# Four packed block products build the delta rule's 128x128 inverse, which is then applied in one product

## The chip, the core and the metric

The kernel runs on one core of a Trainium2 chip. The core has a matrix engine (TensorE, PE in the profile; its weight loads are listed as PEld), a vector engine (DVE), a scalar engine (ACT), a general one (POOL), and a queue that issues DMAs (SP). Each engine works through its own queue in order, and waits for the others by semaphores. A matrix product reads a stationary operand (the weights, 128 rows by up to 128 columns) and a moving operand from SBUF and writes to PSUM; the other engines bring the result from there to SBUF.

The metric is the device time of one execution in microseconds. Lower is better.

## What is computed

One layer of a hybrid encoder over 256 tokens of width 2048: RMSNorm; a wide input projection that feeds retention (8 heads) and a gated delta rule (16 heads of width 128); gates and an output projection; cross-attention to 256 memory tokens; a squared-ReLU MLP of hidden width 8192; a last RMSNorm. All in float32. The change is inside the delta rule, which the reference states by chunks:

```python
kb = kc * bc
m = jnp.where(strict, jnp.einsum("nbhid,nbhjd->nbhij", kb, kc) * decay, 0.0)
t = lax.linalg.triangular_solve(eye + m, jnp.broadcast_to(eye, m.shape),
                                left_side=True, lower=True, unit_diagonal=True)
u = t @ (vc * bc)
w = t @ (kb * jnp.exp(cum_g)[..., None])
qk = jnp.einsum("nbhid,nbhjd->nbhij", qc, kc) * decay
...
v_new = u_i - w_i @ state
o = (q_i * jnp.exp(g_i)[..., None]) @ state + qk_i @ v_new
```

Put for a whole sequence, each head has to solve a unit lower triangular system (I + M) y = r, where M holds the decayed products of keys, and then to form o from y. The kernel does this with tiles of 128 tokens (two tiles, `NT` = 2).

## The kernel before

**The stream.** Most of the work is products of activations with weights read from HBM. `fetch` (L89 on) loads a piece of weights (`raw`), rounds it on ACT to a high part (`whi`, L108) and takes the rest on DVE (`wlo`, L111), with three buffers of each; `chunk` and `blocks` then issue the products on PE (L151 to L153, and L193 and L194). `blocks` of two output blocks is a run of pairs, one product of 512 columns (L193) and one of 256 (L194).

**The order.** A scheduler with its own model of the engines puts every engine's instructions in order. `fetch` has a high priority there. Work that is not stream is mixed into it: a generator in the list `steps` is advanced by `step()`, twice in each group of weights, up to its next `yield`; `finish_steps()` runs what is left.

**The delta rule.** The loop near the end of the mixer runs over four groups `j` of four heads:

- `gdn_stream(j)` projects q, k, v of the group, forms the products of keys and of queries with keys, and writes them, scaled and decayed, to one tile `alt` for each head (four buffers). `diag(alt)` is the part that lies within a 128-token tile, with M transposed in it. The four 32x32 blocks on the diagonal are copied to `cmp_l`, and the right sides r to `r4`.
- `gdn_blocks(j)` sends `cmp_l` through DRAM so that each of the 32 blocks (4 heads, 2 tiles, 4 blocks) has a partition of its own, inverts them there by 31 steps of forward substitution on DVE (L650, L652), sends them back through DRAM to `ct` (one DMA for each of four groups of 32 partitions, L657), and transposes each block to `cu` (L659). Then DVE spreads them over block-diagonal 128x128 tiles `t0` and `u0` (L667, with the mask `bd32`) and clears the diagonal blocks of `diag(alt)` (L671, with the mask `offd`).
- `gdn_core(j)` is the generator that goes into `steps`. With T the block-diagonal inverse and N = M_off T, where M_off is M without its diagonal blocks, the inverse is T (I - N)(I + N N), since N to the fourth is zero. For each tile it forms N once (L681, copied to `am` on ACT, L682), and then applies N three times and T once to the 128x128 right side of each head: w = N r (copied on ACT, L702), sq = r + N w (DVE, L704), sq = sq - N sq (DVE, L706), y = T sq (ACT, L708). The second tile first has the first one's part taken off (L699). Last, the outputs are formed from y, normalised and scaled for both tiles (L718 to L728).

Each such application goes through `times` (L689): four products, one for each head, of 128 columns, float32. One float32 product stands in the trace as two weight loads and two matrix instructions, so one call of `times` is eight of each. A core has twelve stretches between its `yield`s.

The first core (j = 0) is put into `steps` after its gates, so it runs beside `gdn_stream(1)`; the others run beside their own retention gates. `finish_steps()` in the next `gdn_stream` and before the last gates closes what is still open.

**Other lines that come up.** L374 and L375 build `bd32` on POOL, L377 to L379 build `offd` on DVE; L228 is the first matrix instruction; L593 is a product with a single column (a sum of squares of q); `PAD1` (L36) is an empty tile that moves the addresses behind it in the pool `kv`, which is closed before the mixer's pool `mix` is opened.

Of the kernel before, what the change touches and what calls it, by code (L numbers as in the profile page):

```python
# [10 lines left out]
F32 = mybir.dt.float32  # L11
F32R = mybir.dt.float32r
I32 = mybir.dt.int32
AF = mybir.ActivationFunctionType
ALU = mybir.AluOpType
AX = mybir.AxisListType

P = 128
D = 2048
S = 256  # L20
NT = S // P
# [3 lines left out]
GH, GD = 16, 128  # L25
# [9 lines left out]
PAD1, PAD2 = 8, 80  # L35
# [16 lines left out]
def trunk(ctx: ExitStack, tc: tile.TileContext, x, mem, positions, norm_mix_g, w_in, conv_w, gdn_a_log, gdn_dt_bias,  # L52
          ret_gn_g, gdn_norm_g, w_out, norm_x_g, norm_mem_g, w_xq, w_xkv, w_xo, norm_ffn_g, w_ff1, w_ff2,
          norm_final_g, inv_freq, out):
    nc = tc.nc
    PSUM = bass.MemoryType.PSUM
    act, vec, pool, pe = nc.scalar, nc.vector, nc.gpsimd, nc.tensor
# [14 lines left out]
    def bank():  # L72
        return psp.tile([P, 512], F32, name="b", tag="b", bufs=4)
# [135 lines left out]
    ones = cp.tile([P, P], F32, name="ones")  # L209
# [163 lines left out]
    bd32 = mc.tile([P, 4], F32, name="bd32")  # L373
    pool.affine_select(bd32, ones[:, :4], pattern=[[-32, 4]], compare_op=ALU.is_ge, fill=0.0, base=0, channel_multiplier=1)  # L374
    pool.affine_select(bd32, bd32, pattern=[[32, 4]], compare_op=ALU.is_ge, fill=0.0, base=31, channel_multiplier=-1)  # L375
    offd = mc.tile([P, P], F32, name="offd")
    vec.memset(offd, 0.0)  # L377
    for q in range(3):
        vec.memset(offd[32 * q:32 * q + 32, 32 * q + 32:], 1.0)  # L379

# [161 lines left out]

    def conv_silu(blk, ps, dst):
        acc = mx.tile([P, S], F32, name="acc", tag="acc", bufs=2)
        act.activation(acc, ps, AF.Copy, scale=cw[:, 3, blk:blk + 1])  # L545
        for j in range(2, -1, -1):
            d = 3 - j
            vec.scalar_tensor_tensor(acc[:, d:], ps[:, :S - d], cw[:, j, blk:blk + 1], acc[:, d:],  # L548
                                     op0=ALU.mult, op1=ALU.add)
        act.activation(dst, acc, AF.Silu)  # L550

    def diag(alt):
        return alt.rearrange("p a n -> p (a n)")[:, 0:512].rearrange("p (t n) -> p t n", t=NT)[:, :, 0:P]

    def gdn_stream(grp):
# [3 lines left out]
        for pr in range(2):  # L559
# [52 lines left out]
            for b in range(2):  # L612
# [13 lines left out]

                vps = bank()
# [8 lines left out]
    def gdn_blocks(heads, cmp_l):  # L636
# [17 lines left out]
        nc.sync.dma_start(scr_t, tw.rearrange("p i c -> p (i c)"))  # L654
        ct = mx.tile([P, 8, 32], F32, name="ct", tag="cmp", bufs=1)
        for q in range(4):
            nc.sync.dma_start(ct[32 * q:32 * q + 32], scr_t[8 * q:8 * q + 8, :].rearrange("g (i c) -> i g c", i=32))  # L657
        cu = mx.tile([P, 8, 32], F32, name="cu", tag="cu", bufs=1)
        vec.transpose(cu.rearrange("p g c -> p (g c)"), ct.rearrange("p g c -> p (g c)"))  # L659

        def big(nm, tag):
            return mx.tile([P, 4, NT, P], F32, name=nm, tag=tag, bufs=1)

        t0, u0, am = big("t0", "g_a"), big("u0", "g_b"), big("am", "g_c")
        for i in range(4):
            for dst, src in ((t0, ct), (u0, cu)):
                vec.tensor_mul(dst[:, i].rearrange("p t (q c) -> p t q c", q=4),  # L667
                               src[:, 2 * i:2 * i + 2, :].unsqueeze(2).to_broadcast([P, NT, 4, 32]),
                               bd32.unsqueeze(1).unsqueeze(3).to_broadcast([P, NT, 4, 32]))
            lo = diag(heads[i])  # L670
            vec.tensor_mul(lo, lo, offd.unsqueeze(1).to_broadcast([P, NT, P]))  # L671
        return t0, u0, am

    def gdn_core(t0, u0, am, heads, r4, qe4, yg):


        for t in range(NT):
            ps = bank()
            pv = ps.rearrange("p (h n) -> p h n", h=4)
            for i in range(4):  # L680
                pe.matmul(pv[:, i, :], t0[:, i, t, :], diag(heads[i])[:, t, :], start=True, stop=True)  # L681
            act.activation(am[:, :, t, :], pv, AF.Copy)  # L682
        yield

        def times(lhs, rhs):
            ps = bank()
            pv = ps.rearrange("p (h n) -> p h n", h=4)
            for i in range(4):
                pe.matmul(pv[:, i, :], lhs(i), rhs[:, i, :], start=True, stop=True)  # L689
            return pv  # L690

        def tmp(nm):
            return mx.tile([P, 4, GD], F32, name=nm, tag="g_" + nm, bufs=1)

        y = mx.tile([P, 4, NT, P], F32, name="y", tag="g_a", bufs=1)
        for t in range(NT):
            rhs = r4[:, :, t, :]
            if t:
                vec.tensor_sub(rhs, rhs, times(lambda i: heads[i][:, 0, P:S], y[:, :, 0, :]))  # L699
                yield  # L700
            w, sq = tmp("w"), tmp("sq")
            act.activation(w, times(lambda i: am[:, i, t, :], rhs), AF.Copy)  # L702
            yield
            vec.tensor_add(sq, rhs, times(lambda i: am[:, i, t, :], w))  # L704
            yield
            vec.tensor_sub(sq, sq, times(lambda i: am[:, i, t, :], sq))  # L706
            yield
            act.activation(y[:, :, t, :], times(lambda i: u0[:, i, t, :], sq), AF.Copy)  # L708
            yield
# [3 lines left out]
        for t in range(NT):  # L713
# [13 lines left out]
            for i in range(4):  # L727
                vec.scalar_tensor_tensor(yg[:, t, i * GD:(i + 1) * GD], ops[:, i * GD:(i + 1) * GD], ro[:, t, i:i + 1],  # L728
                                         gdng, op0=ALU.mult, op1=ALU.mult)
            yield  # L730

# [338 lines left out]
```

## Time and profile before

| | |
|---|---|
| median of three runs | 2099.76 us (2099.24 to 2100.12) |
| the profiled execution | 2099.76 us, of which the span of the trace is 2098.0 us |
| mean granted TensorE clock | 0.999 |
| HBM read and written | 390.40 MB and 13.65 MB |
| first and last product of a core, in the four groups | 374.3 to 428.7, 555.4 to 616.2, 771.7 to 832.8, 993.5 to 1056.4 us |

The page of the profile gives each engine's busy time, the busy tenths of 40 slices, the chain of work that ended last, and the costliest groups of instructions with their mean duration and the idle time before them. A matrix instruction's duration includes its way through the array, and the next one starts before it ends; so what an instruction costs is read from the distance between starts, in the timeline, and not from its duration.

### The profile page before, as it was taken

The numbers are of one execution on the slowest core, as the hardware profiler recorded it, in microseconds if no ns is written. First come the engines' busy times: TensorE is split into PE (matmuls) and PEld (weight loads), VectorE is DVE, ScalarE is ACT, GpSimd is POOL, SyncE is SP. The second block draws the span as 40 slices with busy tenths as digits, with TensorE's granted clock in tenths as the row PEclk, the third lists the DMA queues.
The fourth block names the chain that finished last, engine by engine and source line by source line (L and its number), as shares of the span: only waits on it lengthen the run. The fifth ranks groups of instructions, "written<-read, shape, count | busy, mean of one in ns | idle before, by whom it ended". The sixth has DMA issues, their size and how long they took to land.

```text
span 2098.0 us, 28725 instructions
## 1 busy us (share of the span) xinstructions
PE 2081.5 (99%) x11172; PEld 1797.4 (86%) x11172; DVE 1407.9 (67%) x2217; ACT 1090.9 (52%) x1700; POOL 28.7 (1%) x39
## 2 busy tenths in 40 slices
PE   8999999999999999999999999999999999999998
PEld 6888888888888888888888899888888888888887
DVE  5766788778758885878557666766556555645655
ACT  7674664565446444655456555554434434444444
POOL 0000000000000000000000000000000000000000
PEclk9999999999999999999999999999999999999999
DMA  8787655556555655555458665566566556656653
GB/s 297 242 272 250 198 188 189 164 172 194 180 162 183 193 179 157 188 186 189 160 177 257 193 187 156 177 199 194 188 200 185 198 189 192 192 190 199 185 198 141
DMA packets 314169, 405.91 MB, mean 193 GB/s; under 512 B 16288, under 2 KB 222128, under 8 KB 313904
## 3 DMA queue, kind: packets, MB, share of 16 engines
q1 hardware_dynamic: 313744, 403.55, 60.7%
q8 instruction: 87, 1.43, 0.3%
q10 hardware_dynamic: 288, 0.52, 0.1%
q14 instruction: 50, 0.41, 0.1%
HBM read 390.40 MB, written 13.65 MB: 193 GB/s over the span
## 4 chain that ended last, share of the span: by engine, by line
PE 95%; DMA 2%; ACT 1%; SPq 1%; DVE 1%; issue 0%; POOLq 0%; POOL 0%; ACTq 0%
PE s L193 33%; PE s L194 17%; PE s L152 13%; PE s L153 13%; PE s L151 13%; PE b L689 2%; DMA xt_d<-xt 1%; DMA xc<-x 1%; PE b L595 1%; ACT whi L108 1%; PE b L121 0%; PE b L123 0%; PE b L122 0%; SPq L292 0%; DVE wlo L111 0%
## 5 line engine op out<-in xcount | busy, mean ns | idle before, releaser
L111 DVE TENSOR_TENSOR wlo<-raw,whi 128x1024 fp32r<-128x1024 f32 x702 | 858.1, 1223 | 525.4 <-ACT whi L108 519.0
L108 ACT ACTIVATE whi<-raw 128x1024 fp32r<-128x1024 f32 x702 | 742.8, 1059 | 739.2 <-PE s L153 388.0
L193 PE MATMUL s<-q,whi 128*128 128x512 f32 x3088 | 1062.8, 390 | 0.3 <-DVE q L959 0.3
L194 PE MATMUL s<-q,wlo 128*128 128x256 f32 x3088 | 845.2, 281 | 0.8 <-DVE wlo L111 0.8
L193 PEld LDWEIGHTS s<-q,whi 128*128 128x128 f32 x3088 | 570.9, 188 | 110.0 <-DVE q L959 0.5
L194 PEld LDWEIGHTS s<-q,wlo 128*128 128x128 f32 x3088 | 579.3, 188 | 14.0 <-DVE wlo L111 2.4
L152 PE MATMUL s<-wlo,q 128*128 128x512 f32 x1264 | 495.3, 392 | 1.4 <-DVE wlo L111 1.3
L153 PE MATMUL s<-whi,q 128*128 128x512 f32 x1264 | 493.0, 390 | 0.0
L151 PE MATMUL s<-whi,q 128*128 128x512 f32 x1264 | 453.3, 391 | 1.5 <-ACT q L255 1.5
L152 PEld LDWEIGHTS s<-wlo,q 128*128 128x128 f32 x1264 | 237.6, 188 | 50.9 <-DVE wlo L111 3.4
L151 PEld LDWEIGHTS s<-whi,q 128*128 128x128 f32 x1264 | 237.2, 188 | 50.6 <-ACT q L255 1.9
L153 PEld LDWEIGHTS s<-whi,q 128*128 128x128 f32 x1264 | 237.7, 188 | 48.1
L200 ACT ACTIVATE bo<-s 128x256 f32<-128x256 f32 x193 | 73.1, 379 | 120.3 <-PE s L194 107.3
L201 DVE TENSOR_TENSOR bo<-bo,s 128x256 f32<-128x256 f32 x193 | 80.3, 416 | 46.4 <-ACT bo L200 46.1
L548 DVE SCALAR_TENSOR_TENSOR acc<-bo,cw,acc 128x255 f32<-128x255 f32 (+2 forms) x144 | 66.8, 479 | 1.5
L650 DVE TENSOR_TENSOR pr<-lw,tw 32x31 f32<-32x31 f32 (+15 forms) x124 | 40.4, 326 | 8.8 <-DMA lw<-scr_l 6.9
L652 DVE TENSOR_TENSOR tw<-tw,pr 32x31 f32<-32x31 f32 (+15 forms) x124 | 40.6, 327 | 2.1
L796 ACT ACTIVATE gth<-s 128x512 f32<-128x512 f32 x32 | 18.9, 592 | 23.8 <-PE s L153 18.3
L998 DVE SCALAR_TENSOR_TENSOR res<-s,rstd3q,res 128x512 f32<-128x512 f32 (+1 forms) x32 | 22.3, 735 | 11.7 <-PE s L153 11.7
L987 DVE SCALAR_TENSOR_TENSOR hs<-bo 128x256 f32<-128x256 f32 x64 | 26.9, 421 | 1.1
L990 DVE TENSOR_TENSOR q<-hs,q 128x256 fp32r<-128x256 f32 x64 | 26.9, 420 | 0.8 <-ACT q L989 0.8
L545 ACT ACTIVATE acc<-bo,cw 128x256 f32<-128x256 f32 x48 | 24.1, 503 | 4.5 <-DVE bo L201 4.4
(292 smaller groups left out, 1083.6 us busy)
## 6 DMA issues: line engine op xcount, KB each, us to landing
raw<-w_in SPq DMA_DIRECT2D x144, 1024.0 KB, 5.2
raw<-w_ff SPq DMA_DIRECT2D x128, 1024.0 KB, 5.4
raw<-w_xkv SPq DMA_DIRECT2D x31, 1024.0 KB, 9.2
raw<-w_out SPq DMA_DIRECT2D x16, 1024.0 KB, 6.1
raw<-w_xq SPq DMA_DIRECT2D x16, 1024.0 KB, 6.6
raw<-w_xo SPq DMA_DIRECT2D x16, 1024.0 KB, 5.2
dec_d<-dec_w SPq DMA_DIRECT2D x8, 384.0 KB, 4.6
dec<-dec_d SPq DMA_DIRECT2D x8, 384.0 KB, 3.2
```

Source lines behind the costliest of these rows:

```text
L108: rounding = act.activation(hi, src, AF.Copy)
L111: vec.tensor_sub(lo, src, hi.bitcast(F32))
L151: pe.matmul(o, xh, wh, start=first, stop=False)
L152: pe.matmul(o, xh, wl, start=False, stop=False)
L153: pe.matmul(o, xl, wh, start=False, stop=last)
L193: pe.matmul(ps[b], lh, xhl, start=kk == 0, stop=False)
L194: pe.matmul(ps[b][:, :S], ll, xh, start=False, stop=kk == KT - 1)
L200: act.activation(o, ps[b][:, S:], AF.Copy)
L201: vec.tensor_add(o, o, ps[b][:, :S])
L548: vec.scalar_tensor_tensor(acc[:, d:], ps[:, :S - d], cw[:, j, blk:blk + 1], acc[:, d:], op0=ALU.mult, op1=ALU.add)
L652: vec.tensor_sub(tw[:, j + 1:32, 0:j + 1], tw[:, j + 1:32, 0:j + 1], pv)
L689: pe.matmul(pv[:, i, :], lhs(i), rhs[:, i, :], start=True, stop=True)
```

## The change

`gdn_blocks` no longer builds the masked tiles `t0`, `u0` and no longer clears blocks of `alt`; `bd32` and `offd` go. The blocks come back from DRAM in another order: the 128 partitions of `ct` hold four pairs of neighbouring blocks (two tiles, two pairs in each), the first block of the pair in the first four columns of blocks and the second one in the last four, one for each head.

The inverse of a lower triangular matrix of two by two blocks, with A and B on the diagonal and C below, has the inverses A' and B' on its diagonal and -B' C A' below. The new core uses that twice. `pair32` holds the four blocks C (transposed) of a head on its diagonal, copied there in `gdn_stream` by ACT. The first call of the new function `couple` forms C A' for all of them, with 32 moving columns for each head; the result is put back on the diagonal of `pair32`; the second call forms the transpose of B' C A', again of 32 columns. It is negated, transposed by blocks of 32 and copied into `t64`, `u64` and `u128`, which hold the inverses of 64x64 blocks (plain and transposed) and the transposed inverse of 128x128. The third and fourth calls do the same with `pair64`, of 64 columns, and fill the last quarter of `u128`. The five new tiles are cleared once when the mixer's pool is opened, and keep their zeros.

Each tile's y is then one `times` with `u128`. The outputs of the first tile are formed right after the second tile's right side is ready. A core has eight stretches between `yield`s in place of twelve.

`PAD1` grows from 8 to 144 columns.

```diff
-PAD1, PAD2 = 8, 80
+PAD1, PAD2 = 144, 80
...
-    bd32 = mc.tile([P, 4], F32, name="bd32")
-    pool.affine_select(bd32, ones[:, :4], pattern=[[-32, 4]], compare_op=ALU.is_ge, fill=0.0, base=0, channel_multiplier=1)
-    pool.affine_select(bd32, bd32, pattern=[[32, 4]], compare_op=ALU.is_ge, fill=0.0, base=31, channel_multiplier=-1)
-    offd = mc.tile([P, P], F32, name="offd")
-    vec.memset(offd, 0.0)
-    for q in range(3):
-        vec.memset(offd[32 * q:32 * q + 32, 32 * q + 32:], 1.0)
...
+    def sparse(nm, *shape):
+        t = mx.tile([P, 4, *shape], F32, name=nm, bufs=1)
+        vec.memset(t, 0.0)
+        return t
+
+    pair32, pair64 = sparse("pair32", P), sparse("pair64", P)
+    t64, u64, u128 = sparse("t64", 64), sparse("u64", 64), sparse("u128", NT, P)
...
+                for t in range(NT):
+                    for a in range(2):
+                        to, at = 64 * t + 32 * a, 64 * a
+                        act.activation(pair32[to:to + 32, slot, to:to + 32],
+                                       diag(alt)[at:at + 32, t, at + 32:at + 64], AF.Copy)
+                    act.activation(pair64[64 * t:64 * t + 64, slot, 64 * t:64 * t + 64], diag(alt)[0:64, t, 64:P], AF.Copy)
...
-        for q in range(4):
-            nc.sync.dma_start(ct[32 * q:32 * q + 32], scr_t[8 * q:8 * q + 8, :].rearrange("g (i c) -> i g c", i=32))
+        for t in range(NT):
+            for a in range(2):
+                at = 64 * t + 32 * a
+                nc.sync.dma_start(ct[at:at + 32], scr_t[16 * a + t:16 * a + 16:2, :].rearrange("g (i c) -> i g c", i=32))
...
-        t0, u0, am = big("t0", "g_a"), big("u0", "g_b"), big("am", "g_c")
-        for i in range(4):
-            for dst, src in ((t0, ct), (u0, cu)):
-                vec.tensor_mul(dst[:, i].rearrange("p t (q c) -> p t q c", q=4),
-                               src[:, 2 * i:2 * i + 2, :].unsqueeze(2).to_broadcast([P, NT, 4, 32]),
-                               bd32.unsqueeze(1).unsqueeze(3).to_broadcast([P, NT, 4, 32]))
-            lo = diag(heads[i])
-            vec.tensor_mul(lo, lo, offd.unsqueeze(1).to_broadcast([P, NT, P]))
-        return t0, u0, am
+        for t in range(NT):
+            for w in range(2):
+                at, to, col = 64 * t, 64 * t + 32 * w, slice(32 * w, 32 * w + 32)
+                vec.tensor_copy(t64[to:to + 32, :, col], ct[at:at + 32, 4 * w:4 * w + 4, :])
+                vec.tensor_copy(u64[to:to + 32, :, col], cu[at + 32:at + 64, 4 * w:4 * w + 4, :])
+                for a in range(2):
+                    at, to = 64 * t + 32 * a, 64 * a + 32 * w
+                    act.activation(u128[to:to + 32, :, t, to:to + 32], cu[at:at + 32, 4 * w:4 * w + 4, :], AF.Copy)
+        return ct, cu
...
+        def couple(lhs, rhs, n):
+            ps = bank()[:, :4 * n]
             pv = ps.rearrange("p (h n) -> p h n", h=4)
             for i in range(4):
-                pe.matmul(pv[:, i, :], t0[:, i, t, :], diag(heads[i])[:, t, :], start=True, stop=True)
-            act.activation(am[:, :, t, :], pv, AF.Copy)
+                pe.matmul(pv[:, i, :], lhs[:, i, :], rhs[:, i, :], start=True, stop=True)
+            return ps, pv
+
+        ps, pv = couple(pair32, ct[:, 0:4], 32)
+        for at in range(0, P, 32):
+            (act.copy if at < 64 else vec.tensor_copy)(pair32[at:at + 32, :, at:at + 32], pv[at:at + 32])
+        yield
+        ps, pv = couple(pair32, cu[:, 4:8], 32)
+        nu = mx.tile([P, 2, P], F32, name="nu", tag="g_w", bufs=1)
+        vec.tensor_scalar(nu[:, 0], ps, -1.0, None, op0=ALU.mult)
+        vec.transpose(nu[:, 1], nu[:, 0])
+        uv, tv = (nu[:, e].rearrange("p (h n) -> p h n", h=4) for e in range(2))
+        for t in range(NT):
+            at = 64 * t
+            vec.tensor_copy(t64[at + 32:at + 64, :, 0:32], tv[at:at + 32])
+            vec.tensor_copy(u64[at:at + 32, :, 32:64], uv[at + 32:at + 64])
+            for a in range(2):
+                act.activation(u128[64 * a:64 * a + 32, :, t, 64 * a + 32:64 * a + 64],
+                               uv[at + 32 * a:at + 32 * a + 32], AF.Copy)
+        yield
+        ps, pv = couple(pair64, t64, 64)
+        for at in range(0, P, 64):
+            (vec.tensor_copy if at else act.copy)(pair64[at:at + 64, :, at:at + 64], pv[at:at + 64])
+        yield
+        ps, pv = couple(pair64, u64, 64)
+        act.activation(u128[0:64, :, 0, 64:P], pv[0:64], AF.Copy, scale=-1.0)
+        vec.tensor_scalar(u128[0:64, :, 1, 64:P], pv[64:P], -1.0, None, op0=ALU.mult)
         yield
...
         for t in range(NT):
             rhs = r4[:, :, t, :]
             if t:
                 vec.tensor_sub(rhs, rhs, times(lambda i: heads[i][:, 0, P:S], y[:, :, 0, :]))
+                outputs(0)
                 yield
-            w, sq = tmp("w"), tmp("sq")
-            act.activation(w, times(lambda i: am[:, i, t, :], rhs), AF.Copy)
-            yield
-            vec.tensor_add(sq, rhs, times(lambda i: am[:, i, t, :], w))
-            yield
-            vec.tensor_sub(sq, sq, times(lambda i: am[:, i, t, :], sq))
-            yield
-            act.activation(y[:, :, t, :], times(lambda i: u0[:, i, t, :], sq), AF.Copy)
+            act.activation(y[:, :, t, :], times(lambda i: u128[:, i, t, :], rhs), AF.Copy)
             yield
+        outputs(1)
+        yield
```

`outputs(t)` is the former body of the loop over tiles that forms o, its norm and `yg`, unchanged.

More of the change, by code (lines that the diff above doesn't have):

```diff
@@ L659, in gdn_blocks @@
         vec.transpose(cu.rearrange("p g c -> p (g c)"), ct.rearrange("p g c -> p (g c)"))
-        def big(nm, tag):
-            return mx.tile([P, 4, NT, P], F32, name=nm, tag=tag, bufs=1)
-        t0, u0, am = big("t0", "g_a"), big("u0", "g_b"), big("am", "g_c")
-        for i in range(4):
-            for dst, src in ((t0, ct), (u0, cu)):
-                vec.tensor_mul(dst[:, i].rearrange("p t (q c) -> p t q c", q=4),
-                               src[:, 2 * i:2 * i + 2, :].unsqueeze(2).to_broadcast([P, NT, 4, 32]),
-                               bd32.unsqueeze(1).unsqueeze(3).to_broadcast([P, NT, 4, 32]))
-            lo = diag(heads[i])
-            vec.tensor_mul(lo, lo, offd.unsqueeze(1).to_broadcast([P, NT, P]))
@@ L672, in gdn_blocks @@
-        return t0, u0, am
-    def gdn_core(t0, u0, am, heads, r4, qe4, yg):
-        for t in range(NT):
-            ps = bank()
+        for t in range(NT):
+            for w in range(2):
[5 more added lines that the diff above has]
+                    act.activation(u128[to:to + 32, :, t, to:to + 32], cu[at:at + 32, 4 * w:4 * w + 4, :], AF.Copy)
@@ L679, in gdn_core @@
+        return ct, cu
+    def gdn_core(ct, cu, heads, r4, qe4, yg):
+        def couple(lhs, rhs, n):
+            ps = bank()[:, :4 * n]
             pv = ps.rearrange("p (h n) -> p h n", h=4)
             for i in range(4):
-                pe.matmul(pv[:, i, :], t0[:, i, t, :], diag(heads[i])[:, t, :], start=True, stop=True)
-            act.activation(am[:, :, t, :], pv, AF.Copy)
+                pe.matmul(pv[:, i, :], lhs[:, i, :], rhs[:, i, :], start=True, stop=True)
[24 more added lines that the diff above has]
+        vec.tensor_scalar(u128[0:64, :, 1, 64:P], pv[64:P], -1.0, None, op0=ALU.mult)
@@ L690, in times @@
             return pv
-        def tmp(nm):
-            return mx.tile([P, 4, GD], F32, name=nm, tag="g_" + nm, bufs=1)
         y = mx.tile([P, 4, NT, P], F32, name="y", tag="g_a", bufs=1)
[L696 to L699, printed above, removed]
-                yield
-            w, sq = tmp("w"), tmp("sq")
-            act.activation(w, times(lambda i: am[:, i, t, :], rhs), AF.Copy)
-            yield
-            vec.tensor_add(sq, rhs, times(lambda i: am[:, i, t, :], w))
-            yield
-            vec.tensor_sub(sq, sq, times(lambda i: am[:, i, t, :], sq))
-            yield
-            act.activation(y[:, :, t, :], times(lambda i: u0[:, i, t, :], sq), AF.Copy)
-            yield
         qe = mx.tile([P, NT, 4], F32, name="qe", tag="qe", bufs=1)
@@ L712, in gdn_core, with outputs @@
         ro = mx.tile([P, NT, 4], F32, name="ro", tag="ro", bufs=1)
-        for t in range(NT):
+        def outputs(t):
             ops = bank()
@@ L729, in gdn_core @@
                                          gdng, op0=ALU.mult, op1=ALU.mult)
+        for t in range(NT):
+            rhs = r4[:, :, t, :]
+            if t:
+                vec.tensor_sub(rhs, rhs, times(lambda i: heads[i][:, 0, P:S], y[:, :, 0, :]))
+                outputs(0)
+                yield
+            act.activation(y[:, :, t, :], times(lambda i: u128[:, i, t, :], rhs), AF.Copy)
             yield
+        outputs(1)
+        yield
     def retention(j, yr):
```

## The prediction

> **What bounds the kernel now.** I read the page first: the engines' shares and the chain of work that ended last.
>
> ```profile
> span 2098.0 us, 28725 instructions
> PE 2081.5 (99%) x11172; PEld 1797.4 (86%) x11172; DVE 1407.9 (67%) x2217; ACT 1090.9 (52%) x1700; POOL 28.7 (1%) x39
> ...
> PE 95%; DMA 2%; ACT 1%; SPq 1%; DVE 1%; issue 0%; POOLq 0%; POOL 0%; ACTq 0%
> ```
>
> PE is on the chain for 95% of the span, and the next engine is busy for 67%. A busy PE is not yet a PE that never waits, so the second view is that of PE's waits, with the line waiting, the releaser, the sum, the count and the longest in us.
>
> ```profile
> PE b L228 <- DMA grow<-norm_mem_g: 2.6, 1, 2.6
> PE b L242 <- DMA xc<-mem: 2.4, 2, 1.6
> PE s L151 <- ACT q L255: 1.5, 1, 1.5
> PE s L152 <- DVE wlo L111: 1.3, 3, 0.6
> PE s L194 <- DVE wlo L111: 0.8, 2, 0.4
> PE s L193 <- DVE q L959: 0.3, 1, 0.3
> ```
>
> These are all: 8.9 us of 2098, and the same view cut to 200 to 1070 us, where the delta rule lies, has no row. So in the region of the change the end is set by how many matrix instructions PE has and how far apart they start. What PE no longer issues there comes off the end in full, if nothing new makes it wait.
>
> The third view gives the room of the others, by stretches: here the first core's, with the busy us of PE, PEld, DVE, ACT and POOL, the granted clock, the DMA share and GB/s.
>
> ```profile
> 374.00:432.00 58.00, 58.00 (x377) 52.62 (x376) 39.53 (x68) 32.05 (x62) 2.01 (x2) 1.00 0.50 155
> ```
>
> PE fills all 58 us; DVE has 18.5 us free, ACT 26, the DMA engines half.
>
> **The price of a product.** Distances between starts are read from the timeline of PE (start, length, instructions merged).
>
> ```profile
> 378.55 0.39 PE L193 MATMUL s<-q,whi 128*128 128x512 f32 x1
> 378.79 0.28 PE L194 MATMUL s<-q,wlo 128*128 128x256 f32 x1
> 378.90 0.39 PE L193 MATMUL s<-q,whi 128*128 128x512 f32 x1
> 379.13 0.28 PE L194 MATMUL s<-q,wlo 128*128 128x256 f32 x1
> 379.25 0.40 PE L193 MATMUL s<-q,whi 128*128 128x512 f32 x1
> 379.49 1.05 PE L689 MATMUL b<-r,am 128*128 128x128 f32 x8
> 380.29 0.36 PE L194 MATMUL s<-q,wlo 128*128 128x256 f32 x1
> 380.50 0.40 PE L193 MATMUL s<-q,whi 128*128 128x512 f32 x1
> ```
>
> An undisturbed pair of L193 and L194 takes 0.35 us (378.55 to 378.90, and to 379.25). With a call of `times` in it the pair takes 379.25 to 380.50, that is 1.25: the call costs 1.25 - 0.35 = **0.90 us**, 0.113 for each of its eight instructions of 128 columns.
>
> The new products have 32 and 64 moving columns. The trace has none such, but it has the product of one column (L593), two of which are four instructions.
>
> ```profile
> 254.60 0.39 PE L193 MATMUL s<-q,whi 128*128 128x512 f32 x1
> 254.82 0.28 PE L194 MATMUL s<-q,wlo 128*128 128x256 f32 x1
> 254.94 0.40 PE L193 MATMUL s<-q,whi 128*128 128x512 f32 x1
> 255.18 0.50 PE L593 MATMUL b<-ones,sq 128*128 128x1 f32 x4
> 255.54 0.36 PE L194 MATMUL s<-q,wlo 128*128 128x256 f32 x1
> 255.74 0.39 PE L193 MATMUL s<-q,whi 128*128 128x512 f32 x1
> ```
>
> 254.94 to 255.74 is 0.80, less a pair of 0.34: 0.46 for four, or 0.114 each. One column costs what 128 cost. The reason is in the weight loads, of which each instruction has one of 128 columns:
>
> ```profile
> L593 PEld LDWEIGHTS b<-ones,sq 128*128 128x128 f32 x64 | 9.3, 191 | 0.9
> L689 PEld LDWEIGHTS b<-w,am 128*128 128x128 f32 x64 | 8.4, 191 | 0.6
> ```
>
> Both last 191 ns, and both groups have a load for each instruction; the stationary operand of `couple` is 128 wide too. So I price a narrow product between a share of 0.113 by columns (32/128 gives 0.028, 64/128 gives 0.056) and 0.114, and take 0.113: the row of one column lies on the far side of both widths, and it is at the upper end. The shorter moving operand gains nothing.
>
> The Trainium skill ("TensorE: Matmul & The Clock Gate", Back-to-back issue gap) gives an isolated instruction of 1 to 64 columns about 60 cycles and one of 128 columns 134. By that alone a couple would cost 60/134 of a call, an estimate of 0.40 us, and the sixteen would cost 6.4 us. L593 speaks against it here: 0.114 us at one column. The same page (LDWEIGHTS) has the load's time depend on its columns only, 128/1.2 = 107 ns, and that is near the 0.113.
>
> **The change, part by part. On PE:**
>
> ```profile
> L681 PE MATMUL b<-alt,t 128*128 128x128 f32 x64 | 8.1, 275 | 0.0
> L689 PE MATMUL b<-r,am 128*128 128x128 f32 x64 | 8.4, 275 | 0.0
> L689 PE MATMUL b<-w,am 128*128 128x128 f32 x64 | 8.4, 275 | 0.0
> L689 PE MATMUL b<-sq,am 128*128 128x128 f32 x64 | 8.4, 275 | 0.0
> ```
>
> These four groups go, 4 x 64 = 256 instructions, or 32 calls of eight: 256 x 0.113 = 28.9 us. (The products with `u0` become the ones with `u128`; those of L699 and the outputs stay.) Four couples in each of four groups come, of eight instructions: 16 x 8 = 128 instructions, at 0.113 14.5 us; by the lower end 64 x 0.028 + 64 x 0.056 = 5.4 us. Net: 128 instructions fewer, 128 x 0.113 = **14.5 us less**; by the lower end 23.5 less.
>
> **On ACT and DVE:**
>
> ```profile
> L111 DVE TENSOR_TENSOR wlo<-raw,whi 128x1024 fp32r<-128x1024 f32 x702 | 858.1, 1223 | 525.4 <-ACT whi L108 519.0
> ...
> L625 ACT ACTIVATE cmp_l<-alt 32x64 f32<-32x64 f32 x64 | 16.0, 250 | 0.6
> L682 ACT ACTIVATE am<-b 128x512 f32<-128x512 f32 x8 | 4.6, 596 | 9.0 <-PE b L681 9.0
> L702 ACT ACTIVATE w<-b 128x512 f32<-128x512 f32 x8 | 4.7, 591 | 5.7 <-PE b L689 5.7
> L667 DVE TENSOR_TENSOR t<-ct,bd 128x256 f32<-128x256 f32 x16 | 5.5, 408 | 0.0
> L671 DVE TENSOR_TENSOR alt<-alt,offd 128x256 f32<-128x256 f32 x16 | 6.7, 419 | 0.0
> L704 DVE TENSOR_TENSOR sq<-r,b 128x512 f32<-128x512 f32 x8 | 5.5, 683 | 3.5 <-PE b L689 3.5
> L650 DVE TENSOR_TENSOR pr<-lw,tw 32x31 f32<-32x31 f32 x8 | 1.4, 178 | 7.0 <-DMA lw<-scr_l 6.9
> L659 DVE STREAM_TRANSPOSE cu<-ct 128x256 f32<-128x256 f32 x4 | 1.8, 445 | 5.0 <-DMA ct<-scr_t 4.8
> L644 DVE MEMSET tw<- 32x1024 f32 x4 | 3.6, 912 | 2.1 <-DMA kt_d<-ko 1.0 <-DMA scr_t<-tw 0.8
> ```
>
> A group gains 40 small instructions on ACT (24 copies into `pair32` and `pair64`, 8 into `u128` in `gdn_blocks`, 8 in the core), at 250 ns as L625 about 10 us, and loses four of 0.59 (L682, L702): 7.6 us more, 30 us over the four groups. Most of it falls into `gdn_stream`, outside the core. DVE loses 8 x 0.41 (L667, both tiles) + 4 x 0.42 + 4 x 0.68 (L704 and its twin L706) = 7.7 us in a group and gains 18 instructions: between 0.18 (L650) and 0.45 (L659) each, 3.2 to 8.0, and I take 0.25, the row of 32 partitions on ACT, so 4.5 us. Clearing the five tiles is 2560 columns once, at L644's 0.9 ns a column 2.3 us. None of it is on the chain: PE's waits on `wlo` sum to 2.1 us in the whole run, and ACT and DVE have 26 and 18.5 us free in the 58 us above. I take zero, and no gain from DVE's relief either. Without that cover (ACT filled, `whi` late) all of ACT's 30 us would show.
>
> **Moved, and the rest.** `ct` still comes by four DMAs on SP of the same 128-byte pieces, at the same place in the queue: zero. `bd32` leaves POOL's queue at the start, and the first product waits there for `grow` as well (2.6 us, above), so nothing is won. The larger `PAD1` makes up for the columns that leave the pool before it; the mixer's tiles move to other addresses, and what they read from there has no price of its own in the trace. The stream's operands lie in pools opened earlier and stay where they are; and the four groups of the core above, with operands at different addresses, all have 275 ns. So I take zero.
>
> **The new waits.** Each couple needs what ACT and DVE made of the one before: after the first and the last two a copy or two, after the second the longest chain (negate, at most L667's 0.41; transpose, at most 0.45; four copies of 0.25 on each engine). A couple that waits holds up every stream product behind it in PE's queue; a DVE or ACT instruction that waits for it holds up `wlo` or `whi` behind it. The old core had the same kind of step twelve times in a group (ACT's `am` waited 9.0 us in total for PE, DVE's `sq` 3.5) and PE waited for none of them: the scheduler puts stream products between one call and the next. Eight steps in place of twelve should fit. I take zero.
>
> **Sum.** The profiled execution is 2099.76 us, 1.8 more than its span, and equals the median. 2099.8 - 14.5 = **2085.3 us**. What this kernel's measurement can tell from no change is about 0.2%, 4.2 us.
>
> **Rivals.**
>
> - **Narrow products are cheaper**, by columns: 2099.8 - 23.5 = 2076.3. The four L593 starts are against it, and so is the load of 128 columns. By the Trainium skill's 60 cycles (the same page and section as above) it would be 2077.3, an estimate. Chance 4%.
> - **The second couple's chain is late now and then**: 0.41 + 0.45 + 4 x 0.25 and one `wlo` of 1.22 us in front (L111) are 3.1 us, four times 12; half of it exposed is 6: about 2091. For it: this chain is longer than any old step. Against: no PE wait in the region. Chance 10%.
> - **The stream cannot use what PE frees**, since weights come at their own pace: then 2099.8, no change. Against: the DMA share of 0.50, and ACT and DVE with a third to a half free, while PE waits for neither. Chance 5%.
> - **Slower: every couple waits on PE's queue for its operands**, because the scheduler's model takes the small cross-partition copies and the transpose as shorter than they are, and places the couple too early. Price in a group: 1.7 (two copies of 0.25 behind a `wlo`) + 3.1 + 1.6 + 1.6 (a copy of 0.41 behind a `wlo`) = 8 us, 32 in all: 2085.3 + 32 = 2117. It makes the kernel slower by more than 0.2% from (14.5 + 4.2) / 16 = 1.2 us a couple on. Against: the same scheduler places the old steps without a wait. Chance 6%.
>
> That the change does not do what it says is ruled out by the code: the four groups of products have no successor.
>
> **How the numbers follow.** The forecast itself has 75%, with its own range 2083 to 2088 (0.90 or 0.91 a call, and small new gaps of a few tenths of us). Faster by over 0.2% (below 2095.6): 75 + 4 + 10 = 89%; within 0.2%: 5%; slower: 6%. The range, for 8 in 10, takes the forecast's and most of the second rival's: 2082.5 to 2092.
>
> **What would show it.** PE's instructions fall from 11172 to 11044. The couples, in the timeline, take 0.9 us between two stream products, as `times` did; 0.2 or 0.4 would be the first rival. PE's waits stay without a row between 200 and 1070 us; rows `b` of the core's lines waiting for ACT or DVE would be the second or the last, and rows `s` waiting for `wlo` the third. The prediction is wrong if the span drops by much other than 128 x 0.113 with PE's waits unchanged.

## The result and the profile after

| | before | after |
|---|---|---|
| median of six runs | 2099.15 us | 2085.16 us |
| lowest and highest | 2098.20 to 2100.12 | 2084.04 to 2086.05 |
| ratio to before, 95% interval | | 0.9931 [0.9922, 0.9941] |
| the profiled execution | 2099.76 us | 2084.04 us |

The changed kernel is 14.0 us faster by the medians; 2085.3 was forecast. Two executions of kernels below, one with the couples' products doubled and one with the late copies made four times, ran at a granted clock of 0.556 and 0.78 and took 3496.67 and 3806.88 us, and the medians given here leave them out. First the engines' shares and the chain that ended last, on the page after the change:

```profile
span 2082.3 us, 28611 instructions
PE 2066.1 (99%) x11044; PEld 1783.3 (86%) x11044; DVE 1402.3 (67%) x2226; ACT 1120.3 (54%) x1844; POOL 30.7 (1%) x37
...
PE 97%; DMA 1%; ACT 1%; SPq 1%; DVE 0%; issue 0%; POOLq 0%; POOL 0%; ACTq 0%; DVEq 0%
```

PE has 128 instructions fewer, and it is still the bound. ACT works 29.4 us more (1090.9 to 1120.3; 30 was said), DVE 5.6 us less. All of PE's waits, in the view of who waited for whom:

```profile
PE b L228 <- DMA grow<-norm_mem_g: 2.6, 1, 2.6
PE b L242 <- DMA xc<-mem: 2.3, 2, 1.5
PE s L151 <- ACT q L255: 1.6, 1, 1.6
PE s L194 <- DVE wlo L111: 0.8, 2, 0.5
PE s L152 <- DVE wlo L111: 0.7, 1, 0.7
PE s L193 <- DVE q L986: 0.3, 1, 0.3
```

They are the same six, and cut to 200 to 1070 us the view is empty again. No couple waits and none makes the stream wait. What one costs is read from the timeline of PE, as it was for `times`:

```profile
377.94 0.39 PE L193 MATMUL s<-q,whi 128*128 128x512 f32 x1
...
378.28 0.39 PE L193 MATMUL s<-q,whi 128*128 128x512 f32 x1
378.51 0.28 PE L194 MATMUL s<-q,wlo 128*128 128x256 f32 x1
378.63 0.97 PE L689 MATMUL b<-cu,pair 128*128 128x32 f32 x8
379.44 0.47 PE L193 MATMUL s<-q,whi 128*128 128x512 f32 x1
379.75 0.28 PE L194 MATMUL s<-q,wlo 128*128 128x256 f32 x1
379.87 0.40 PE L193 MATMUL s<-q,whi 128*128 128x512 f32 x1
```

A pair takes 377.94 to 378.28, 0.34 us. From 378.28 to 379.87 there are two pairs and the couple: 1.59 less 0.69 is 0.90 us, for eight instructions of 32 columns. The third couple, with 64 columns, takes 385.05 to 386.30 with its pair: 1.25 less 0.35, again 0.90.

Where in the run did the time go? Two places show it, each with the first and last start of a product that both kernels have: the sums of squares of q, in the four `gdn_stream`s, and the column sums after the mixer. Of each pair of rows the first is from the kernel before and the second from the changed one.

```profile
L593 PE MATMUL b<-ones,sq x64: 164/250/250, 250.0 to 912.4; 128*128 128x1 f32 x64
L899 PE MATMUL b<-ones,acc x8: 167/251/251, 1190.8 to 1393.8; 128*128 128x2 f32 x8
```

```profile
L594 PE MATMUL b<-ones,sq x64: 164/250/250, 248.7 to 900.3; 128*128 128x1 f32 x64
L926 PE MATMUL b<-ones,acc x8: 167/251/251, 1174.7 to 1377.7; 128*128 128x2 f32 x8
```

Ahead of the first core the changed kernel is 1.3 us early (250.0 to 248.7), after the last core 16.1 (1190.8 to 1174.7), and at 1393.8 still 16.1. So the four cores gave 16.1 - 1.3 = 14.8 us, against 128 x 0.113 = 14.5, and nothing was won or lost behind them. The 1.3 us at the start is a difference between two executions, not one of the kernels: in runs below with the same code up to there, this product first starts at 249.1 (the narrow products in turn), 249.6 (the copies later), 249.7 (the narrow products in a row) and 251.7 us (the late copies four times). The profiled executions lie 15.7 us apart for that reason and the medians 14.0.

### The profile page after: what moved, and what is told of

Its sections match the earlier page's. It is cut to its first block, busy times and chain, and to the rows that moved or that the text cites. A ratio compares the mean times of both kernels' runs of the same rounds, so it can differ in the third digit from the quotient of the medians.

```text
span 2082.3 us, 28611 instructions
## 1 busy us (share of the span) xinstructions
PE 2066.1 (99%) x11044; PEld 1783.3 (86%) x11044; DVE 1402.3 (67%) x2226; ACT 1120.3 (54%) x1844; POOL 30.7 (1%) x37
## 4 chain that ended last, share of the span: by engine, by line
PE 97%; DMA 1%; ACT 1%; SPq 1%; DVE 0%; issue 0%; POOLq 0%; POOL 0%; ACTq 0%; DVEq 0%
PE s L193 33%; PE s L194 17%; PE s L152 14%; PE s L151 14%; PE s L153 14%; PE b L689 1%; PE b L596 1%; DMA xc<-x 1%; PE b L722 1%; PE b L122 0%; PE b L121 0%; PE b L123 0%; SPq L292 0%; ACT dec_w L501 0%; PE b L598 0%
## 5 line engine op out<-in xcount | busy, mean ns | idle before, releaser
L193 PE MATMUL s<-q,whi 128*128 128x512 f32 x3088 | 1062.4, 390 | 0.3 <-DVE q L986 0.3
L194 PE MATMUL s<-q,wlo 128*128 128x256 f32 x3088 | 845.0, 281 | 0.8 <-DVE wlo L111 0.8
L193 PEld LDWEIGHTS s<-q,whi 128*128 128x128 f32 x3088 | 570.7, 188 | 110.5 <-DVE q L986 0.5
L194 PEld LDWEIGHTS s<-q,wlo 128*128 128x128 f32 x3088 | 579.2, 188 | 14.3 <-DVE wlo L111 2.7
L549 DVE SCALAR_TENSOR_TENSOR acc<-bo,cw,acc 128x255 f32<-128x255 f32 (+1 forms) x144 | 66.8, 479 | 3.1 <-ACT acc L546 1.2
L1016 ACT ACTIVATE q<-hs 128x256 fp32r<-128x256 f32 x64 | 26.2, 410 | 0.0
```

The lines of the kernel that those rows point to most:

```text
L193: pe.matmul(ps[b], lh, xhl, start=kk == 0, stop=False)
L194: pe.matmul(ps[b][:, :S], ll, xh, start=False, stop=kk == KT - 1)
```

## The experiments

The theory at this point: what the change saves is a number of PE instructions, each with a load of 128 columns of weights and at most 128 moving columns, at 0.113 us each, and everything else is covered. Its rivals: the width of the moving operand counts, the load does not, or the other engines' work has a price. All kernels are variants of the changed one; the ratios are to the kernel before, measured beside it, with 95% intervals.

### Moving columns: 128 in place of 32 and 64

`rhs(i)` is a stretch of 128 columns of the same tile that holds the wanted ones, and the copies take these.

```diff
-                pe.matmul(pv[:, i, :], lhs[:, i, :], rhs[:, i, :], start=True, stop=True)
+                pe.matmul(pw[:, i, :], lhs[:, i, :], rhs(i), start=True, stop=True)
...
```

(the lines left out pick the wanted columns out of `pw`, with four copies more in a core)

> Each couple's four products take 128 moving columns in place of 32 or 64; the surplus columns are not used, and the copies of the third and fourth couple become four more in a core. Theory (an instruction costs what its 128-column weight load costs, 0.113 us, whatever the moving width up to 128): a couple still costs 0.90 us between stream products, and the time stays at 2085 +- 1.5 us, ratio to the kernel before 0.993. Rival (the cost goes with the moving columns, so that the change's narrow products were part of the gain): 64 instructions at 0.085 us more and 64 at 0.057 more, 9 us, so 2094, ratio 0.9975, and a couple would now cost visibly more than in the changed kernel.

Measured: 2085.47 us, ratio 0.9935 [0.9920, 0.9950]. PE's timeline in that kernel, at the third couple:

```profile
386.03 0.39 PE L193 MATMUL s<-q,whi 128*128 128x512 f32 x1
386.26 1.05 PE L688 MATMUL b<-t,pair 128*128 128x128 f32 x8
387.07 0.36 PE L194 MATMUL s<-q,wlo 128*128 128x256 f32 x1
387.27 0.39 PE L193 MATMUL s<-q,whi 128*128 128x512 f32 x1
```

386.03 to 387.27 is 1.24, less a pair 0.90 us: the same couple with twice the columns. The narrow moving operand bought nothing; the first rival is out.

### The number: each couple's products twice

```diff
             for i in range(4):
-                pe.matmul(pv[:, i, :], lhs[:, i, :], rhs[:, i, :], start=True, stop=True)
+                for _ in range(2):
+                    pe.matmul(pv[:, i, :], lhs[:, i, :], rhs[:, i, :], start=True, stop=True)
```

> Each product of a couple is issued twice into the same place: 128 matrix instructions more, 11172 again as before the change, with everything else as changed. Theory (the whole gain is 128 instructions fewer at 0.113 us): 14.5 us more, 2099.6, ratio 1.000 to the kernel before, a couple costs 1.8 us. Rival (part of the gain comes from elsewhere, from DVE's relief, fewer steps or the order): clearly under 2099, by as much as that part is.

Measured: 2098.49 us, ratio 0.9997 [0.9987, 1.0006]. With the old number of PE instructions the old time is back. What the change does elsewhere (fewer steps, less work on DVE, more on ACT) is worth 0.6 us by the medians, which is no difference: the interval runs from 2.7 us under the old time to 1.3 us over it.

### The weights: a second product with 32 of the 128 stationary columns

```diff
                 pe.matmul(pv[:, i, :], lhs[:, i, :], rhs[:, i, :], start=True, stop=True)
+                pe.matmul(pv[0:32, i, :], lhs[:, i, 0:32], rhs[:, i, :], start=True, stop=True)
```

> After each product of a couple the same one again with only the first 32 of the 128 stationary columns, so it writes the first 32 rows again: 128 instructions more, as many as when all are doubled, but with weight loads of a quarter. Theory (the weight load's columns set the cost): 32/128 of 0.113 is 0.028 us, the moving columns 32 and 64 by their share 0.028 and 0.056, so 3.6 to 5.4 us more, 2089 to 2091. Rival (a fixed cost of any float32 instruction, whatever it loads): 14.5 us more, 2099.6.

Measured: 2105.97 us, ratio 1.0032 [1.0020, 1.0043], which is 20.8 us more. Both expectations missed: a product with a quarter of the weights costs more than a whole one. Its weight loads are short all the same. The loads of this kernel, whole and narrow, busy us and mean ns, and then PE's timeline at the second couple:

```profile
L689 PEld LDWEIGHTS b<-cu,pair 128*128 128x128 f32 x32 | 5.1, 188 | 0.8
L690 PEld LDWEIGHTS b<-cu,pair 128*32 128x32 f32 x32 | 2.2, 108 | 0.7
```

```profile
380.53 0.41 PE L689 MATMUL b<-cu,pair 128*128 128x32 f32 x2
380.87 0.25 PE L690 MATMUL b<-cu,pair 128*32 128x32 f32 x2
381.05 0.41 PE L689 MATMUL b<-cu,pair 128*128 128x32 f32 x2
```

The load is 80 ns shorter for 96 columns less, 0.83 ns a column, so a 128-column load has 107 ns that go with its columns. But from one pair of whole products to the next it is 0.52 us (380.53 to 381.05) where two whole instructions take 0.23: a narrow pair costs 0.29, and it comes with two changes between a whole and a narrow array. With 64 moving columns (388.31 to 388.91, in the third couple) it is 0.60 and 0.37. The narrow product writes again where the whole one has just written, but that is not the reason: the doubled products did so too, at (2098.49 - 2085.16) / 128 = 0.104 us each. That suggests that the change of width costs, and the next run tells it apart.

### The same, four whole products first and then four narrow ones

```diff
             for i in range(4):
                 pe.matmul(pv[:, i, :], lhs[:, i, :], rhs[:, i, :], start=True, stop=True)
+            for i in range(4):
+                pe.matmul(pv[0:32, i, :], lhs[:, i, 0:32], rhs[:, i, :], start=True, stop=True)
```

> As with the extra products of 32 stationary columns, which cost 20.8 us, 0.147 us an instruction with 32 moving columns and 0.186 with 64: but first all four full products of a couple and then the four narrow ones, so the width of the weights changes twice in a couple and not eight times. Theory now (a narrow load is cheap by its columns, 0.028 us, and each change of width costs: (4 x 0.295 - 8 x 0.028) / 8 = 0.12 us): 8 x 0.028 + 2 x 0.12 = 0.46 us for a couple of 32 columns, and with 64, 8 x 0.056 + 2 x 0.13 = 0.71; 9.4 us in all, 2094.6. Rival (a narrow load is itself slow): again 20 us, 2105.

Measured: 2095.03 us, ratio 0.9978 [0.9969, 0.9987], 9.9 us more than the changed kernel, with 9.4 expected. PE's timeline:

```profile
379.77 0.39 PE L193 MATMUL s<-q,whi 128*128 128x512 f32 x1
380.00 0.97 PE L689 MATMUL b<-cu,pair 128*128 128x32 f32 x8
380.91 0.44 PE L691 MATMUL b<-cu,pair 128*32 128x32 f32 x8
...
381.50 0.39 PE L193 MATMUL s<-q,whi 128*128 128x512 f32 x1
```

379.77 to 381.50 is 1.73, less a pair (0.35) and the couple (0.90): 0.48 us for eight narrow instructions and two changes of width, 0.46 expected. The kernel with the products in turn has eight changes for as many narrow instructions and pays 4 x 0.29 = 1.16. The six changes more cost 0.68, so a change costs about 0.11 us, and what is left of the 0.48 is 0.03 for a narrow instruction. With 64 moving columns (386.67 to 388.61 in this kernel, less a pair and a couple, 0.70 us) the same working gives 0.13 and 0.05: once the load is narrow, the moving columns count. So a narrow load is cheap, and each change of the width in use costs about 0.12 us. The Trainium skill ("TensorEngine Tiling (Array Packing)", Key Properties) says that a change of the tiling mode drains the engine; these two runs agree with it if a product with 32 stationary columns is such a mode, which no trace here shows. A single narrow product between whole ones doesn't pay, then; by these figures a row pays from about three instructions on, an estimate (two changes, 0.22 us, against 0.08 saved by each).

### One float32 product where one pass is enough

If the price is the load, the cheapest target is the sum of squares of q, one column at full price and, in float32, two instructions for each product. Rounded squares do there, since the sum only scales a term of 1e-6.

```diff
-                sq = mx.tile([P, S], F32, name="sq", tag="acc", bufs=2)
+                sq = mx.tile([P, S], F32R, name="sq", tag="acc", bufs=2)
...
-                    pe.matmul(ssq[:, b, t:t + 1], sq[:, t * P:(t + 1) * P], ones[:, :1], start=True, stop=True)
+                    pe.matmul(ssq2[:, b, t], sq[:, t * P:(t + 1) * P], ones_r, start=True, stop=True)
```

> The sums of squares of q (products with one column) take the squares and the column of ones in fp32r, two equal columns, so a product is one weight load and one matrix instruction and not two; the squares are rounded, they only scale a term of 1e-6 under a root. Theory (each 128-column load costs 0.113 us, however little moves): 32 instructions fewer, 3.6 us, so 2081.5, ratio 0.9916. Rival (an instruction of one column is so short that it hides beside its neighbours): 2085, ratio 0.9933.

Measured: 2081.72 us, ratio 0.9917 [0.9903, 0.9930]; 3.4 us under the changed kernel where 3.6 was expected. The page's line of that kernel:

```profile
PE 2063.6 (99%) x11012; PEld 1779.8 (86%) x11012; DVE 1401.3 (67%) x2226; ACT 1120.3 (54%) x1845; POOL 30.7 (1%) x37
```

32 instructions fewer than 11044. This version beats both kernels; the interval still overlaps the changed kernel's, but the size is the one the theory gives.

### The steps: no yields between the couples

```diff
             (act.copy if at < 64 else vec.tensor_copy)(pair32[at:at + 32, :, at:at + 32], pv[at:at + 32])
-        yield
         ps, pv = couple(pair32, cu[:, 4:8], 32)
```

(and the same after the second and third couple)

> The yields after the first three couples are taken out, so all four couples and the copies between them are one stretch of the core. Theory (the scheduler, which knows that a couple's operands are not ready, puts stream products between the couples anyway): 2085 +- 2 us, and the couples stand some microseconds apart as before. Rival (the yields keep the couples apart, and without them a couple at the head of PE's queue holds the stream up): by the prediction's price 8 us in a group, 2085 + 32 = 2117, and PE's waits get rows of the couple's line released by ACT or DVE.

Measured: 2085.45 us, ratio 0.9935 [0.9920, 0.9950], no row of L689 among PE's waits. The couples of the first core still start 6 to 7 us apart, in PE's timeline of that kernel:

```profile
379.66 1.03 PE L689 MATMUL b<-cu,pair 128*128 128x32 f32 x8
...
386.37 1.00 PE L689 MATMUL b<-t,pair 128*128 128x64 f32 x8
```

It is the scheduler that keeps dependent products apart, and the yields are not needed for it. The rival on the slow side, a couple at the head of PE's queue waiting for its copies, has no support even where it was invited.

### The pad

```diff
-PAD1, PAD2 = 144, 80
+PAD1, PAD2 = 8, 80
```

> PAD1 back to 8 columns, so the tiles behind it in the pool kv lie 544 bytes lower than before the change and after it; nothing else. Theory (no product before the mixer depends on the address): 2085 +- 1.5 us. Rival (the change of PAD1 keeps a clash of addresses away that would slow the first 200 us): more than 1.5 us above, and all of the difference ahead of the first core.

Measured: 2085.86 us, ratio 0.9936 [0.9924, 0.9949]. The address has no price that can be measured here.

### ACT's copies, doubled

```diff
-                        act.activation(pair32[to:to + 32, slot, to:to + 32],
-                                       diag(alt)[at:at + 32, t, at + 32:at + 64], AF.Copy)
+                        for _ in range(2):
+                            act.activation(pair32[to:to + 32, slot, to:to + 32],
+                                           diag(alt)[at:at + 32, t, at + 32:at + 64], AF.Copy)
```

(and the same for `pair64`)

> ACT's 24 copies in a group from the products of keys into the two block-diagonal tiles are made twice: 96 more ACT instructions, 0.225 us (32x32) and 0.256 (64x64) each in the changed kernel's trace, 22.6 us of ACT. Theory (ACT is off the path, PE never waits for it in the delta rule): 2085 +- 1.5 us, no new row of PE's waits. Rival (the change gave back part of what PE saved through ACT): up to 22.6 us more, anything above 2088 would show it.

Measured: 2094.92 us, ratio 0.9980 [0.9971, 0.9990]: 9.8 us more. The theory missed: ACT is not off the path without limit. PE's waits in this kernel have grown from 1.5 to 6.3 us for `wlo`, the first two rows of the view:

```profile
PE s L194 <- DVE wlo L111: 3.4, 7, 0.5
PE s L152 <- DVE wlo L111: 2.9, 6, 0.8
```

They grew by 4.8 us, which is half of the 9.8. The view counts idle time, and a late start is idle time only from the listed end of the instruction before it. PE's timeline shows one such start and, ahead of it, the same instructions undisturbed:

```profile
261.55 0.62 PE L193 MATMUL s<-q,whi 128*128 128x512 f32 x2
262.01 0.40 PE L194 MATMUL s<-q,wlo 128*128 128x256 f32 x2
...
264.37 0.73 PE L193 MATMUL s<-q,whi 128*128 128x512 f32 x2
265.63 0.51 PE L194 MATMUL s<-q,wlo 128*128 128x256 f32 x2 [0.53 <-DVE wlo L111]
```

From the two L193 to the two L194 it is 0.46 us undisturbed and 1.26 here: 0.80 us are lost where the row has 0.53. All of the 9.8 us lies in the mixer: from the first sum of squares of q to the first column sum this kernel takes 935.8 us (249.4 to 1185.2), the changed one 926.0 (248.7 to 1174.7).

DVE's `wlo` for this start began at 264.35, after 2.77 us of waiting for ACT's `whi`. ACT's timeline in this kernel, over three roundings of weights, shows why (the rows between are copies and other small work of the heads):

```profile
252.46 1.05 ACT L108 ACTIVATE whi<-raw 128x1024 fp32r<-128x1024 f32 x1
...
256.21 1.04 ACT L108 ACTIVATE whi<-raw 128x1024 fp32r<-128x1024 f32 x1
...
263.26 1.06 ACT L108 ACTIVATE whi<-raw 128x1024 fp32r<-128x1024 f32 x1
```

In the changed kernel the same stretch is shorter:

```profile
251.68 1.05 ACT L108 ACTIVATE whi<-raw 128x1024 fp32r<-128x1024 f32 x1
...
254.87 1.06 ACT L108 ACTIVATE whi<-raw 128x1024 fp32r<-128x1024 f32 x1
...
260.99 1.06 ACT L108 ACTIVATE whi<-raw 128x1024 fp32r<-128x1024 f32 x1
```

Without gaps ACT works at small instructions from one `whi` to the next, 3.2 and 6.1 us from start to start in the changed kernel and 3.8 and 7.1 in this one. PE uses such a half of a piece of weights up in eight pairs, 2.8 us, and three are buffered. The changed kernel's 9.3 us over the two are bridged without a wait; this one's 10.8 are not.

### Is it that place?

The first idea was that only this place in `gdn_stream` is short of ACT. The second set was put at the end of `gdn_blocks`:

> The second set of ACT's 24 copies in a group is made once more, as where they were doubled in place (which cost 9.8 us), but at the end of gdn_blocks, after the blocks have come back, and not in the middle of gdn_stream. The number of ACT instructions and their work are the same as there. Theory (what counts is the queue of small ACT instructions between two roundings of weights at one place in gdn_stream, not ACT's load): 2085 +- 2 us, and no waits of PE for wlo beyond those of the changed kernel. Rival (96 more ACT instructions cost what they cost wherever they stand): again about 2095.

Measured: 2094.69 us, ratio 0.9979 [0.9969, 0.9988]. It tells nothing, since the copies did not move. The view of the tiles `pair` in that kernel, with first and last start:

```profile
L631 ACT ACTIVATE pair<-alt x64: 212/227/230, 254.2 to 915.2; 32x32 f32<-32x32 f32 x64
L684 ACT ACTIVATE pair<-alt x64: 208/227/230, 254.9 to 917.3; 32x32 f32<-32x32 f32 x64
```

The scheduler issued the second set (L684) among the first (L631), as soon as their data was there. So the next kernel repeats copies that cannot start early, those from `cu`:

```diff
-                    act.activation(u128[to:to + 32, :, t, to:to + 32], cu[at:at + 32, 4 * w:4 * w + 4, :], AF.Copy)
+                    for _ in range(4):
+                        act.activation(u128[to:to + 32, :, t, to:to + 32], cu[at:at + 32, 4 * w:4 * w + 4, :], AF.Copy)
```

> ACT's eight copies in a group from cu into the transposed 128x128 inverse (308 ns each in the changed kernel's trace) are made four times: again 24 more ACT instructions in a group, 7.4 us of ACT a group, 30 us in all, more than the 22.6 us of the doubled copies in gdn_stream. They can't start before the blocks have come back from DRAM, so the scheduler can't put them into gdn_stream, as it did with the last kernel's, which stood in the same windows as the doubled ones (254 to 265 us and so on). Theory (the place counts: between the grams and the right sides ACT has no room left, elsewhere it has): 2085 +- 2 us. Rival (ACT's added load costs wherever it stands, 9.8 us for 22.6): about 13 us more, 2098.

Measured: 2094.50 us, ratio 0.9979 [0.9969, 0.9989], so 9.3 us more: the idea of the one place falls, and the rival's 13 us is too much as well. The stalls have moved along with the copies. One start of PE, the `wlo` that it waits for, and ACT's timeline around them, in that kernel:

```profile
387.00 0.51 PE L194 MATMUL s<-q,wlo 128*128 128x256 f32 x2 [0.52 <-DVE wlo L111]
385.72 1.23 DVE L111 TENSOR_TENSOR wlo<-raw,whi 128x1024 fp32r<-128x1024 f32 x1 [2.81 <-ACT whi L108]
```

```profile
372.34 1.06 ACT L108 ACTIVATE whi<-raw 128x1024 fp32r<-128x1024 f32 x1
...
379.66 1.06 ACT L108 ACTIVATE whi<-raw 128x1024 fp32r<-128x1024 f32 x1
...
384.63 1.06 ACT L108 ACTIVATE whi<-raw 128x1024 fp32r<-128x1024 f32 x1
385.60 2.62 ACT L679 ACTIVATE u<-cu 32x128 f32<-32x128 f32 x8
388.24 1.06 ACT L108 ACTIVATE whi<-raw 128x1024 fp32r<-128x1024 f32 x1
```

This `wlo` comes from the `whi` of 384.63. Between the roundings ahead of it lie mostly copies, 7.3 us (372.34 to 379.66) and 5.0 (to 384.63), and the next one follows after eight copies, 3.6 us, while PE uses one up in 2.8. So no single run need be longer than what the buffers hold: small instructions on ACT are dear wherever they stand, once the roundings fall further behind PE's use of them than the buffered weights bridge.

### The same copies on POOL

Two kernels put copies on POOL, which is busy for 1%: the second set there with ACT's own kept, and the only set there.

```diff
-                        act.activation(pair32[to:to + 32, slot, to:to + 32],
-                                       diag(alt)[at:at + 32, t, at + 32:at + 64], AF.Copy)
+                        pool.tensor_copy(pair32[to:to + 32, slot, to:to + 32],
+                                         diag(alt)[at:at + 32, t, at + 32:at + 64])
```

(the second of the two kernels; in the first one the POOL copy stands ahead of ACT's; `pair64` likewise)

> The second set of the 24 copies in a group from the products of keys is issued on POOL, ahead of ACT's, and not on ACT; the same bytes are written twice. Theory (the 10 us of the doubled copies come from ACT's queue, where weights wait for their rounding behind a run of small instructions, and not from the copies as such): 2085 +- 2 us, no new waits of PE for wlo. Rival (more small copies between the same tiles cost by themselves, by waits between the engines or by SBUF traffic, whichever engine makes them): about 2095 again, or more, since ACT's copies now wait for POOL's.

> The 24 copies in a group from the products of keys are made on POOL in place of ACT, once. Theory (with one set ACT just has room, so the change's own copies cost nothing): 2085 +- 1.5 us, as on ACT. Rival (they already delay the weights a little, 9.8 us for a second set suggests some for the first): below 2083.5.

Measured: a second set on POOL 2087.36 us, ratio 0.9945 [0.9930, 0.9960]; the only set on POOL 2085.11, ratio 0.9935 [0.9919, 0.9952]. POOL's copies are slower than ACT's, in the groups of the first of the two:

```profile
L631 POOL COPY pair<-alt 32x32 f32<-32x32 f32 x64 | 19.9, 310 | 6.5 <-DVE alt L618 2.2 <-DVE alt L621 1.1 <-ACT acc L546 0.4
```

Most of the 9.8 us goes away when the second set leaves ACT's queue, so for that part it was that queue. The 2.2 us that stay lie a little outside of what was expected. Part of the rival is seen here: ACT's own copies wait for POOL's, 3.2 us in all, once 1.13 us just ahead of a rounding of weights, and PE has waits of 1.1 us for `wlo` between 200 and 1070 us, where the changed kernel has none.

```profile
256.11 0.26 ACT L636 ACTIVATE pair<-alt 64x64 f32<-64x64 f32 x1 [1.13 <-POOL pair L635]
256.28 1.04 ACT L108 ACTIVATE whi<-raw 128x1024 fp32r<-128x1024 f32 x1
```

The second kernel bears on the question that the doubled copies had raised: taking the change's own copies off ACT wins nothing. Alone it doesn't show that they cost nothing, since copies on POOL may have a price too. With the changed kernel's trace, which has no wait of PE between 200 and 1070 us, no cost of theirs is left to be seen; from the first sum of squares to the first column sum the two kernels take the same time (926.3 us with the copies on POOL, 926.0 on ACT).

## Why the prediction was right

- **PE bounds, and freed instructions come off the end in full.** Right: 14.8 us between the first core and the last, 14.0 between the medians, 14.5 forecast. Doubling the couples' products gave it back (2098.49).
- **A narrow product costs what a whole one costs, 0.113 us.** Right, and for the reason given: 0.90 us a couple with 32, 64 and 128 moving columns; the load's own time goes with its columns (80 ns for 96), and in a row an instruction with a quarter of the load costs 0.03 us. The Trainium skill's 60 cycles for 1 to 64 columns ("TensorE: Matmul & The Clock Gate", Back-to-back issue gap) are given there for the isolated gap between instructions, and the 0.40 us a couple estimated from them is not what these products, each with a load of 128 columns, take. Its rule on the load (LDWEIGHTS), 128/1.2 = 107 ns, agrees with the 0.113 us and with the 0.83 ns a column.
- **ACT, DVE and the moved pieces cost nothing.** Right in the result: their work changed as said (29.4 us more on ACT for 30; the five tiles were cleared in 2.4 us for 2.3), and a version without the 24 copies on ACT has the same time. The ground given for it was poor, though, so the zero was in part luck. The step that fails is "ACT and DVE have 26 and 18.5 us free in the 58 us above": that stretch is the core's, while the prediction itself puts most of the copies outside it, and what counts is not a mean share but how far ACT's roundings fall behind PE's use of them. There the cover is thin: 1.5 us more over two roundings were too much. The prediction's bound, that without the cover all of ACT's 30 us would show, was too high for what could be tried: 22.6 and 30 us of further copies cost 9.8 and 9.3.
- **The new waits cost nothing.** Right: PE's waits have no row of a couple, even with the yields taken out, and the time leaves no room for one.
- **The pad costs nothing.** Right within 1 us.
- **The rivals.** The narrow product by columns (2076) is refuted by the couples with 128 columns; the late second couple and the waiting couple by PE's waits; the stream that can't use what PE frees by the time itself.

## What to carry to other kernels

Where PE is the bound and every product has its own weights, count weight loads, not columns: a product of one column costs what one of 128 does (0.114 and 0.113 us an instruction here), a float32 one costs two, and a formula that saves columns but not products saves nothing. Don't mix widths of stationary operands in one stream; group them. And before work is called covered, look at how far runs of small instructions put back the pieces of work that the bound needs from that engine, against what is buffered, and not at its mean share.

## What had not been expected of the hardware

A product with 32 stationary columns between two with 128 costs more than another whole one (0.147 us an instruction with 32 moving columns and 0.186 with 64, against 0.113). In a row the narrow ones cost 0.48 us for eight, two changes of width included. So a change of the stationary width costs about 0.12 us here; why is not shown.
